# A streaming-encoder block: the scan stage's TensorE order written out by hand, with the entry reordered

## The chip, the core and the metric

The kernel runs on one core of one Trainium2 chip. The metric is the device time of one execution in microseconds (us): the median of three runs is given, and beside it one execution that was recorded by the hardware profiler. The engines are named as in the profile: PE is TensorE's matmul part, PEld its weight loads, DVE is VectorE, ACT is ScalarE, POOL is GpSimd, and SP is the engine whose queue issues all DMA transfers of this kernel. Each engine executes its own instructions in the order of the program; semaphores hold an instruction back until what it reads or overwrites is ready.

## The reference

One layer on 512 tokens of 1024 channels, all in float32:

- h is a layer norm of x. One projection of h gives z (2048 columns), xbc (3072), dt (32), q (1024), ckv (256), the index query (512), index key (64) and index weight (8), and two gates (1024 each).
- Branch A, the scan. xbc passes a causal depthwise convolution of four taps and SiLU, and is split into xs (32 heads of 64), B and C (4 groups of 128 states). The scan is done in chunks: the product of C and B inside a chunk is weighted by decays exp(a_i - a_j) and applied to xs; chunk states B·xs are carried on with a decay and read by C. The result plus D·xs is gated with SiLU(z), normalised over each group (RMS), and projected to 1024 (w_br_ssd).
- Branch B, the attention. A score of index queries and index keys selects the 128 best keys of each token; 16 heads attend to these keys through a shared latent of 256, with a relative bias.
- Both branches are gated and summed, projected (w_out), added to h and normalised; a convolutional FFN of 2 x 2816 columns and a last layer norm follow.

## The kernel before

**Precision.** A projection in float32 is made of three matmuls on values split in two parts: hi·hi, lo·hi and hi·lo, where hi is the value rounded to the type fp32r and lo the rest. One instruction of 128x128 weights and 512 columns stands for one such product. A weight tile of 128x1024 (one load, 512 KB) is split by ACT (`whi`, L190) and DVE (`wlo`, L191) after its DMA. A projection of 128 output channels over 8 k-tiles of h is so 24 matmuls of 512 columns into one PSUM bank (`proj`, L228). The matmuls inside the scan itself are plain float32 and have 128 columns or one.

**PSUM.** There are eight banks: three `acc` for projections, two `tr` for transposes, and `a`, `b`, `c` for the rest.

**Entry.** Four tiles of x (128 tokens each) are loaded, their mean and variance taken on DVE, normalised (tiles 0 and 1 by two ACT instructions each, L343 and L344; tiles 2 and 3 by DVE, L348), transposed on PE, evicted with the layer norm's gain (L360, L362), and split into `hhi` (L368) and `hlo` (L369). Three projections begin as soon as parts of h are there: the small columns (104: index key, dt, index weight) and the first two tiles of the index query (`his`, L381). A helper `put` fixes the order of DVE, ACT and POOL here, and `chain` fixes PE's order.

**The scan stage** (L702 to L729). After the decays, the latents and the index keys, `scores` multiplies 24 times (3 token blocks, 8 heads) index queries by keys. Then `ssd_in(g)` projects B, C and four xs tiles of a group g with their convolutions; `ssd_core(g, j)` does the scan of one xs tile (two heads): transposes of xs (L597), chunk states (`sp`, L608), the carry on DVE (`pv`, L615), decays on ACT (eight Relu of 128 columns, L621, and one Exp), their product with the masked C·B (L624), the states' part (`yo`, L627, bank `b`), the part within the chunk (`yd`, L631, bank `c`: eight matmuls of 64 output rows, heads in turn on the two halves), and the sum on DVE and POOL (L634 to L636); then z is projected and gates the result. `ssd_norm` and `ssd_out` finish a group while the next is under way. The loops only give the order of the program text: a list scheduler at build time orders each engine's instructions by that text and by its own estimate of when each is ready. Between a projection's 24 matmuls it may so put matmuls of the scan.

**Selection.** `select(i)` (L523) finds the 128 best keys of a token block by 16 rounds of a maximum and a replacement on DVE; its first instruction may not stand ahead of the result `v` of a core named in `PINS`: (2, 2), (3, 1), (3, 3).

After the scan stage come the first pair's q and k, four gates, the last group's output projection (these three in the scheduler's order), the attention in a PE order written by hand, and the output projection and the FFN.

## Time and profile before

| | |
|---|---|
| median of 3 runs | 1116.24 us (1116.22 to 1117.04) |
| the profiled execution | 1116.95 us |
| its span, first to last instruction | 1115.2 us |
| PE busy | 1092.7 us (98%), 5420 matmul instructions |
| PEld busy | 900.8 us (81%) |
| DVE busy | 780.7 us (70%) |
| ACT busy | 479.8 us (43%) |
| POOL busy | 175.3 us (16%) |
| DMA | 125.62 MB, mean 113 GB/s |

The profile's busy time of an engine is the union of its instructions' durations. A matmul's end is modelled, and consecutive ones overlap; the distance from one start to the next is what a matmul costs in a stream. An idle time is given with what ended it ("<-"). PEclk is the share of full clock that TensorE was granted.

### The profile page before, as it was taken

Reading aid. Unit: us, or ns where it says so; the run is one execution under the profiler, and the core shown is the slowest. Engines: PE = TensorE matmul, PEld = TensorE weight load, DVE = VectorE, ACT = ScalarE, POOL = GpSimd, SP = SyncE. Lnnn points to the kernel's source line nnn. Section 1 sums busy time; section 2 is a strip of 40 time slices with the busy share of each in tenths; the row PEclk is TensorE's granted clock in tenths of the full one; section 3 lists DMA queues with packets and bytes.
Section 4 is the critical chain, followed back from the end, with each engine's and each line's share of the span. In section 5 each row is a group of like instructions: output and inputs, shape, how many; then the busy total and the mean of one; then the engine's idle time right before and its main releaser. Section 6 shows DMA issues by size and latency. Waiting matters only on the chain.

```text
span 1115.2 us, 14590 instructions
## 1 busy us (share of the span) xinstructions
PE 1092.7 (98%) x5420; PEld 900.8 (81%) x5420; DVE 780.7 (70%) x1409; ACT 479.8 (43%) x825; POOL 175.3 (16%) x177
## 2 busy tenths in 40 slices
PE   7999999999999999999999999999999999999996
PEld 5888788878888888887777778888888888888885
DVE  7769678856799799758989848666656565542227
ACT  5475646554553423255555524215444444432220
POOL 3000023112211132013232432130000000000002
PEclk9999999999999999999999999999999999999999
DMA  6542343373333332422322356502232233333232
GB/s 234 169 137 78 103 131 116 107 226 132 119 109 123 103 106 85 146 81 71 90 67 75 116 175 187 187 1 95 95 95 95 95 97 101 105 95 95 95 95 76
DMA packets 41640, 125.62 MB, mean 113 GB/s; under 512 B 4720, under 2 KB 9120, under 8 KB 41568
## 3 DMA queue, kind: packets, MB, share of 16 engines
q1 hardware_dynamic: 41568, 124.68, 35.0%
q8 instruction: 43, 0.70, 0.3%
q14 instruction: 29, 0.24, 0.1%
HBM read 118.21 MB, written 9.59 MB: 115 GB/s over the span
## 4 chain that ended last, share of the span: by engine, by line
PE 86%; DVE 6%; DMA 4%; issue 2%; ACT 1%; POOL 1%; SPq 0%; DVEq 0%; ACTq 0%; POOLq 0%
PE pacc L217 52%; PE pc L217 5%; PE pacc L241 5%; PE ptr L241 4%; PE pa L217 3%; PE pb L217 3%; PE pb L241 2%; PE pc L241 2%; PE pa L241 2%; DMA rs_d<-rb_d 1%; DVE wlo L191 1%; PE pc L631 1%; PE ptr L217 1%; DMA G<-ac_d 1%; DMA prow<-in_prow_dram 1%
## 5 line engine op out<-in xcount | busy, mean ns | idle before, releaser
L191 DVE TENSOR_TENSOR wlo<-wraw,whi 128x1024 fp32r<-128x1024 f32 x159 | 203.4, 1279 | 155.3 <-ACT whi L190 154.6
L190 ACT ACTIVATE whi<-wraw 128x1024 fp32r<-128x1024 f32 x159 | 168.0, 1057 | 211.1 <-PE pacc L217 135.1
L217 PE MATMUL pacc<-hhi,whi 128*128 128x512 f32 (+1 forms) x536 | 217.4, 406 | 0.8 <-ACT hhi L368 0.8
L217 PE MATMUL pacc<-hlo,whi 128*128 128x512 f32 (+1 forms) x536 | 212.0, 395 | 1.6 <-DVE hlo L369 1.6
L217 PE MATMUL pacc<-hhi,wlo 128*128 128x512 f32 (+1 forms) x536 | 209.1, 392 | 0.2 <-DVE wlo L191 0.2
L217 PEld LDWEIGHTS pacc<-hlo,whi 128*128 128x128 f32 (+1 forms) x536 | 100.7, 188 | 25.0 <-DVE hlo L369 3.3
L217 PEld LDWEIGHTS pacc<-hhi,whi 128*128 128x128 f32 (+1 forms) x536 | 101.1, 189 | 21.6 <-issue 2.6
L217 PEld LDWEIGHTS pacc<-hhi,wlo 128*128 128x128 f32 (+1 forms) x536 | 100.8, 188 | 19.6 <-issue 0.6
L172 POOL TENSOR_TENSOR rs_y<-rs_v,mhalf 128x1 f32<-128x1 f32 (+1 forms) x14 | 14.0, 1000 | 463.2 <-DVE rs_v L170 463.2
L217 PE MATMUL pacc<-h1hi,wlo 128*128 128x512 f32 (+1 forms) x216 | 79.0, 366 | 0.0
L217 PE MATMUL pacc<-h1hi,whi 128*128 128x512 f32 (+1 forms) x216 | 78.9, 366 | 0.0
L217 PE MATMUL pacc<-h1lo,whi 128*128 128x512 f32 (+1 forms) x216 | 78.7, 366 | 0.0
L814 POOL TENSOR_TENSOR tm<-mask,toe 128x128 f32<-128x128 f32 (+1 forms) x64 | 44.5, 699 | 156.8 <-DVE mn L825 94.5
L636 POOL TENSOR_TENSOR v<-v,eaB 128x384 f32<-128x384 f32 x16 | 22.8, 1424 | 230.4 <-DVE eaB L634 152.6
L548 DVE SCALAR_TENSOR_TENSOR cv<-pacc,cwb,cv 128x509 f32<-128x509 f32 (+2 forms) x72 | 53.3, 741 | 0.6
L621 ACT ACTIVATE G<-G,acT 128x128 f32<-128x128 f32 x128 | 39.4, 389 | 31.5 <-DMA G<-ac_d 30.1
L828 ACT ACTIVATE l<-l,mn 128x128 f32<-128x128 f32 (+1 forms) x64 | 35.7, 558 | 36.9 <-DVE mn L825 35.8
L217 PE MATMUL pacc<-yhi,whi 128*128 128x512 f32 x128 | 51.1, 400 | 0.0
L217 PE MATMUL pacc<-yhi,wlo 128*128 128x512 f32 x128 | 50.2, 392 | 0.0
L217 PE MATMUL pacc<-ylo,whi 128*128 128x512 f32 x128 | 50.1, 392 | 0.0
L217 PEld LDWEIGHTS pacc<-h1hi,whi 128*128 128x128 f32 x216 | 40.8, 189 | 6.7
L217 PEld LDWEIGHTS pacc<-h1hi,wlo 128*128 128x128 f32 x216 | 40.7, 189 | 6.6
(476 smaller groups left out, 2275.0 us busy)
## 6 DMA issues: line engine op xcount, KB each, us to landing
wraw<-in_w_up_dram SPq DMA_DIRECT2D x44, 512.0 KB, 3.5
wraw<-in_w_xbc_dram SPq DMA_DIRECT2D x24, 512.0 KB, 3.5
wraw<-in_w_down_dram SPq DMA_DIRECT2D x22, 512.0 KB, 3.4
wraw<-in_w_z_dram SPq DMA_DIRECT2D x16, 512.0 KB, 3.5
G<-ac_d SPq DMA_DIRECT2D x16, 512.0 KB, 4.0
wraw<-in_w_br_ssd_dram SPq DMA_DIRECT2D x16, 512.0 KB, 3.5
eaB<-ea_d SPq DMA_DIRECT2D x32, 128.0 KB, 3.1
wraw<-in_w_ga_dram SPq DMA_DIRECT2D x8, 512.0 KB, 3.5
```

The costliest lines, as they stand in the source:

```text
L172: last_pow[0] = nc.gpsimd.tensor_tensor(y, v, mhalf[:, :n], OP.pow)
L190: nc.scalar.activation(hi[:, :cols], raw[:, :cols], AF.Copy)
L191: nc.vector.tensor_tensor(lo[:, :cols], raw[:, :cols], hi[:, :cols].bitcast(F32), OP.subtract)
L217: pe(nc.tensor.matmul(p, a, b, start=start, stop=stop).ins)
L241: nc.tensor.matmul(p, x[a][:, tok(i)], w[b][h], start=first and j == 0, stop=last and j == 2)
L548: nc.vector.scalar_tensor_tensor(y[:, d:], p[:, :T - d], cwb[:, 24 * k + c:24 * k + c + 1], y[:, d:], OP.mult, OP.add)
L621: nc.scalar.activation(G[:, h, c], G[:, h, c], AF.Relu, bias=acT[:, c, h0 + h:h0 + h + 1], scale=-1.0)
L631: nc.tensor.matmul(yd[h * 64:(h + 1) * 64, tok(c)], xd[:, c, h], G[:, h, c], start=True, stop=True)
L636: nc.gpsimd.tensor_tensor(v[:, P:], v[:, P:], eaB[:, P:], OP.add)
L814: nc.gpsimd.tensor_tensor(tm[:, :K - f], maskt[i][:, f:], self.toe[:, 2 * P - K + f:], OP.add)
L828: nc.scalar.activation(l[:, :K], l[:, :K], AF.Exp, bias=self.mn[:, ic], scale=-1.0, accum_out=self.sm[:, ic])
```

## The change

**Entry.** The variance's constant and the negated mean times the root of tiles 0 to 2 move from DVE to POOL; tiles 0 to 2 are each normalised by one ACT instruction, tile 3 by DVE. The warming matmuls of PE use a tile of ones instead of x: 20 ahead of the first transposes, two after each of tiles 0 and 1 (before: six on x[1], two on x[2]; a float32 matmul shows as two records). The small weights are padded from 104 to 128 columns for each k-tile (the load grows from 416 to 512 KB) and split in two halves on ACT. The orders of ACT and DVE and of the first three projections on PE are rewritten.

**Scan stage.** The loop over `ssd_core` is replaced by generators for the projections (one step is one k-tile: three matmuls) and by lists of items that are called after given steps; `chain` is on, so PE's order is the order of these calls. Items come for two cores j and j + 1 at once (`pair`). There are nine runs: the first has no pair (48 steps), then come 40, 48, four of 56, 40 and 32; together 432 steps. The decays of a core are issued in four pieces of two Relu (`ssd_g`); the transposes of B (`ssd_b`) stand apart from the product C·B (`ssd_cb`); the parts within the chunk of both cores are one item (`ssd_d`, banks `c` and `a`); the root of a norm (`rms_root`, bank `b`) stands apart from its broadcast (`rms_bcast`, bank `c`). The 24 score products are items too and use the two `tr` banks. Two gates (`out_ga`) move from the last group to the first run. The bias rows' loads (`t5_load`) and product (`t5_rows`) are items of the first run of group 1. The selections' first instructions may follow the cores (1, 3), (2, 3) and (3, 1).

```diff
-PINS = ((2, 2), (3, 1), (3, 3))
-IN_STEPS = (1, 1, 2, 2)
-OUT_STEPS = (0, 0, 0, 2, 4)
...
-        put(V, nc.vector.tensor_scalar(v, mv[:, 1:2], 1.0, EPS, OP.mult, OP.add))
+        if i < 3:
+            put(G, nc.gpsimd.tensor_scalar(v, mv[:, 1:2], 1.0, EPS, OP.mult, OP.add))
+        else:
+            put(V, nc.vector.tensor_scalar(v, mv[:, 1:2], 1.0, EPS, OP.mult, OP.add))
         last_pow[0] = put(G, nc.gpsimd.tensor_tensor(y, v, mhalf[:, :1], OP.pow))
-        if i < 2:
-            put(V, nc.vector.tensor_scalar(nm, mv[:, 0:1], -1.0, None, OP.mult))
+        if i < 3:
+            put(G, nc.gpsimd.tensor_scalar(nm, mv[:, 0:1], y, -1.0, OP.mult, OP.mult))
...
+    def warm(n):
         for _ in range(n):
-            mm(trs[7][:, :P], ident, xt[i][:, :P], start=True, stop=True)
+            mm(trs[7][:, 3 * P:], ones, ones, start=True, stop=True)
+
+    warm(20)
     for i, t in enumerate(xt):
+        if i < 3:
+            put(S, nc.scalar.activation(t, t, AF.Identity, bias=nms[i], scale=rss[i]))
+        else:
+            for j in range(2):
+                x_ = t[:, half_of(j)]
+                put(V, nc.vector.tensor_scalar(x_, x_, mvs[i][:, 0:1], rss[i], OP.subtract, OP.mult))
+        for k in range(KD):
+            mm_t(trs[k][:, tok(i)], t[:, tok(k)], ident)
         if i < 2:
-            put(S, nc.scalar.activation(t, t, AF.Identity, bias=nms[i]))
-            put(S, nc.scalar.activation(t, t, AF.Copy, scale=rss[i]))
-        for j in range(2):
-            x_ = t[:, half_of(j)]
-            if i > 1:
-                put(V, nc.vector.tensor_scalar(x_, x_, mvs[i][:, 0:1], rss[i], OP.subtract, OP.mult))
-            for k in range(4 * j, 4 * j + 4):
-                mm_t(trs[k][:, tok(i)], t[:, tok(k)], ident)
+            warm(2)
         nc.sync.dma_start(htok_d[:, i], t)
...
+    w_hi(0, slice(0, 4))
+    for k in range(2):
         evict(k)
-        evict(k + 1)
-        for j in (k, k + 1):
-            put(S, nc.scalar.activation(hhi[:, j], hfs[j], AF.Copy))
-            put(V, nc.vector.tensor_tensor(hlo[:, j], hfs[j], hhi[:, j].bitcast(F32), OP.subtract))
-        if k < 6:
-            w_hi(1 + k // 2)
-    for j in range(4):
+    h_hi(0)
+    evict(2)
+    h_lo(0)
+    h_hi(1)
+    h_lo(1)
+    w_hi(1)
+    h_hi(2)
+    evict(4)
+    h_lo(2)
+    evict(3)
+    h_hi(3)
+    evict(6)
+    h_lo(3)
+    w_hi(0, slice(4, KD))
+    w_lo(0)
+    h_hi(4)
+    h_lo(4)
+    w_hi(2)
+    evict(5)
+    evict(7)
+    for k in (5, 6, 7):
+        h_hi(k)
+        h_lo(k)
+    w_hi(3)
+    for j in range(1, 4):
         w_lo(j)
...
+    his(0, 0, 1)
+    his(1, 0, 1)
+    for k in (2, 3):
+        his(0, k)
+        his(1, k)
+    los(0, 0, 1, 2, 3)
+    his(0, 4)
+    his(1, 4)
+    his(2, 0, 1, 2)
+    his(0, 5)
+    his(1, 5)
+    his(2, 3, 4, 5)
+    for k in (6, 7):
+        for j in range(3):
+            his(j, k)
+    los(0, 4, 5, 6, 7)
+    los(1, *range(KD))
+    los(2, *range(KD))
     chain[0] = False
...
-                p = any_tile("abc")
-                nc.tensor.matmul(p[:, :K], qi[h][:, tok(i - 1)], khi[:, :K], start=True, stop=False)
-                nc.tensor.matmul(p[:, :K], qi[h][:, tok(i - 1)], klo[:, :K], start=False, stop=True)
+                p = tr_tile()
+                mm(p[:, :K], qi[h][:, tok(i - 1)], khi[:, :K], start=True, stop=False)
+                mm(p[:, :K], qi[h][:, tok(i - 1)], klo[:, :K], start=False, stop=True)
...
+    def in_b(g):
 
         bc = wt("k4", [P, 2, T], "bc")
-        BT, CT = bc[:, 0], bc[:, 1]
-        st_ = {"CT": CT, "xs": []}
-        sins[g] = st_
-        conv_silu(BT, proj_h(w_("w_xbc", 16 + g)), 16 + g)
+        sins[g] = {"BT": bc[:, 0], "CT": bc[:, 1], "xs": [], "core": [], "v": []}
+        p = acc_tile()
+        yield from steps(p, w_("w_xbc", 16 + g), hT)
+        conv_silu(bc[:, 0], p, 16 + g)
         yield
-        conv_silu(CT, proj_h(w_("w_xbc", 20 + g)), 20 + g)
...
+    def in_z(g, j):
+
+        p = acc_tile()
+        yield from steps(p, w_("w_z", 4 * g + j), hT)
+        zs = wt("m2", [P, T], "zs")
+        nc.scalar.activation(zs, p, AF.Tanh, scale=0.5)
+        nc.vector.scalar_tensor_tensor(zs, zs, 1.0, p, OP.add, OP.mult)
+        sins[g]["z", j] = zs
+        ssd_gate(g, j)
+        yield
...
+    def ssd_g(g, j, n):
+
+        G = sins[g]["core", j][2]
+        h, c0 = n // 2, n % 2 * 2
+        q = 2 * (4 * g + j) + h
+        for c in range(c0, c0 + 2):
+            nc.scalar.activation(G[:, h, c], G[:, h, c], AF.Relu, bias=acT[:, c, q:q + 1], scale=-1.0)
+        if n == 3:
+            nc.scalar.activation(G, G, AF.Exp, scale=-1.0)
...
+    def ssd_y(g, j):
...
+            mm(yo[:, tok(c)], pv[:, c - 1], s_["CT"][:, tok(c)], start=True, stop=True)
         nc.vector.tensor_tensor(eaB[:, P:], yo[:, P:], eaB[:, P:], OP.mult)
...
+    def ssd_d(g, js):
+
+        s_ = sins[g]
+        yds = [ps(t) for t in "ca"]
+        for j, yd in zip(js, yds):
+            xd, xdd, G, eaB, pv = s_["core", j]
+            for c in range(NT):
+                for h in range(2):
+                    mm(yd[h * 64:(h + 1) * 64, tok(c)], xd[:, c, h], G[:, h, c], start=True, stop=True)
+        for j, yd in zip(js, yds):
+            q = 4 * g + j
+            eaB = s_["core", j][3]
+            v = wt("v", [P, T], "v")
+            last_v[0] = nc.vector.scalar_tensor_tensor(v, s_["xs"][j], Dv[:, q:q + 1], yd, OP.mult, OP.add)
+            nc.gpsimd.tensor_tensor(v[:, P:], v[:, P:], eaB[:, P:], OP.add)
+            s_["v"].append(v)
+            ssd_gate(g, j)
...
+    AT = (2, 6, 13, 18, 28, 32, 40)
...
+    sins, last_v, pins, ga = {}, [None], [], SSD_GATES
+    score = scores()
+
+    def run(projs, items):
+
+        k = 0
+        for p in projs:
+            for _ in p:
+                for f, *args in items.get(k, ()):
+                    f(*args)
+                k += 1
+        assert k > max(items), (k, items)
+
+    def pair(g, j, at, more=(), root=10, norm=20):
+
+        items = {}
+        more = [*more]
+        if g and not j:
+            more += [(root, ssd_root, g - 1), (norm, ssd_norm, g - 1)]
+        x0, x1, s0, s1, y0, y1, d = at
+        for n in range(4):
+            more += [(x0 + 3 + 2 * n, ssd_g, g, j, n), (x1 + 4 + 2 * n, ssd_g, g, j + 1, n)]
+        more += [(x0, ssd_x, g, j), (x1, ssd_x, g, j + 1), (s0, ssd_s, g, j, "a"), (s1, ssd_s, g, j + 1, "b"),
+                 (s1 + 2, ssd_gm, g, j), (s1 + 5, ssd_gm, g, j + 1),
+                 (y0, ssd_y, g, j), (y1, ssd_y, g, j + 1), (d, ssd_d, g, (j, j + 1))]
+        for k, *f in more:
+            items.setdefault(k, []).append(f)
+        return items
+
+    def scored(*ks):
+        return [(k, next, score, None) for k in ks]
+
+    def pin():
+        pins.append(last_v[0])
+
+    chain[0], last_pe[0] = True, None
+    first_items = {k: [f] for k, *f in scored(*range(33, 48, 2))}
+    first_items[26] = [(ssd_b, 0)]
+    first_items[44] = [(ssd_cb, 0)]
+    run([in_b(0), in_c(0), out_ga(0), in_x(0, 0), out_ga(1), in_x(0, 1)], first_items)
+    run([in_x(0, 2), in_z(0, 0), in_x(0, 3), in_z(0, 1), in_b(1)],
+        pair(0, 0, (2, 10, 14, 19, 26, 29, 36), scored(*range(1, 40, 3))))
+    run([in_x(1, 0), in_x(1, 1), in_z(0, 2), in_c(1), in_z(0, 3), in_x(1, 2)],
+        pair(0, 2, AT, [*scored(3, 5, 7), (21, ssd_b, 1)]))
+    for g in (1, 2):
+        run([in_x(g, 3), in_z(g, 0), in_b(g + 1), in_z(g, 1), out_br(g - 1, 0), out_br(g - 1, 1), in_c(g + 1)],
+            pair(g, 0, AT, [(1, ssd_cb, 1), (18, t5_load), (46, t5_rows)] if g == 1 else ()))
+        run([in_x(g + 1, 0), in_z(g, 2), out_br(g - 1, 2), in_x(g + 1, 1), in_z(g, 3), out_br(g - 1, 3),
+             in_x(g + 1, 2)], pair(g, 2, AT, [(11, ssd_b, g + 1), (21, ssd_cb, g + 1), (42, pin)]))
+    run([in_x(3, 3), in_z(3, 0), in_z(3, 1), out_br(2, 0), out_br(2, 1)],
+        pair(3, 0, (0, 4, 11, 16, 25, 28, 36), [(37, pin)], norm=18))
+    run([in_z(3, 2), in_z(3, 3), out_br(2, 2), out_br(2, 3)],
+        pair(3, 2, (0, 3, 9, 14, 23, 25, 30)))
+    chain[0] = False
```

Left out of the diff: the same move of code from `ssd_in` and `ssd_core` into `in_c`, `in_x`, `out_br`, `out_ga`, `ssd_b`, `ssd_cb`, `ssd_x`, `ssd_gm`, `ssd_s` and `ssd_gate`, with `mm` and `mm_t` in place of direct matmul and transpose calls; `steps` moved up; the padding of the small weights.

## Rows read from the trace of the kernel before

**Rows 1.** The page, part 4: shares of the chain that ended last.
```profile
PE 86%; DVE 6%; DMA 4%; issue 2%; ACT 1%; POOL 1%; SPq 0%; DVEq 0%; ACTq 0%; POOLq 0%
```
**Rows 2.** Stretches: length, busy us and count of each engine, PEclk, DMA.
```profile
56.00:448.00 392.00, 389.06 (x2064) 321.30 (x2063) 314.60 (x544) 196.68 (x366) 73.53 (x55) 1.00 0.38 119
308.00:420.00 112.00, 112.00 (x612) 92.80 (x611) 102.68 (x212) 45.35 (x83) 23.50 (x18) 1.00 0.36 112
```
**Rows 3.** The chain that ended last, in the FFN: start us, us, what.
```profile
785.51 5.44 PE pacc L217 x24
```
**Rows 4.** PE's groups from 56 to 448 us: form, count, busy, mean ns, idle before.
```profile
L217 PE MATMUL pacc<-hhi,whi 128*128 128x512 f32 x358 | 142.4, 398 | 0.0
...
L217 PE MATMUL pacc<-yhi,whi 128*128 128x512 f32 x96 | 38.8, 404 | 0.0
...
L631 PE MATMUL pc<-G,xd 128*64 128x128 f32 x256 | 19.7, 281 | 0.2 <-DVE v L635 0.2
L627 PE MATMUL pb<-bc,pv 128*128 128x128 f32 x96 | 17.8, 282 | 1.6 <-DVE pv L615 1.3 <-ACT pv L611 0.3
L608 PE MATMUL pa<-xdd,bt 128*128 128x128 f32 x96 | 13.3, 275 | 0.0
L597 PE MATMUL ptr<-ident,xs 128*128 128x128 f32 x64 | 9.8, 275 | 0.0
```
**Rows 5.** PE in order of time, one core's matmuls kept together: start, us, what.
```profile
408.18 0.83 PE L608 MATMUL pa<-xdd,bt 128*128 128x128 f32 x6
408.94 1.09 PE L631 MATMUL pc<-G,xd 128*64 128x128 f32 x16
409.96 0.50 PE L217 MATMUL pacc<-hhi,whi 128*128 128x512 f32 x1
410.30 0.39 PE L217 MATMUL pacc<-hhi,wlo 128*128 128x512 f32 x1
```
**Rows 6.** PE in order of time, pieces of several cores mixed.
```profile
233.98 0.87 PE L631 MATMUL pc<-G,xd 128*64 128x128 f32 x10
234.78 0.49 PE L627 MATMUL pb<-bc,pv 128*128 128x128 f32 x2
...
236.65 0.43 PE L631 MATMUL pc<-G,xd 128*64 128x128 f32 x2
...
237.36 0.40 PE L217 MATMUL pacc<-hhi,wlo 128*128 128x512 f32 x1
```
**Rows 7.** PE's waits from 56 to 448 us: total us, times, longest.
```profile
PE pb L627 <- DVE pv L615: 1.3, 1, 1.3
...
PE pc L631 <- DVE v L635: 0.2, 1, 0.2
```
**Rows 8.** Stretches of the entry, columns as in rows 2.
```profile
11.00:14.80 3.80, 3.07 (x26) 2.60 (x24) 2.97 (x7) 2.31 (x5) 0.90 (x1) 1.00 1.00 304
14.80:17.90 3.10, 1.40 (x4) 0.70 (x5) 2.04 (x5) 2.15 (x4) 1.98 (x1) 0.99 1.03 421
17.90:21.30 3.40, 3.40 (x10) 2.41 (x9) 2.37 (x4) 3.02 (x5) 3.40 (x1) 0.50 0.37 152
```
**Rows 9.** The entry in order of time: start, us, what, idle before and what ended it.
```profile
15.81 0.39 DVE L400 COPY Dv<-prow 64x16 f32<-64x16 f32 x2 [1.66 <-DMA prow<-in_prow_dram]
...
16.98 0.48 PE L217 MATMUL pacc<-hlo,whi 128*104 128x512 f32 x1 [1.63 <-DVE hlo L369]
...
32.88 0.33 PE L217 MATMUL pb<-hhi,wlo 128*128 128x384 f32 x1
```
**Rows 10.** Durations ns min/median/max, first and last start, of single lines.
```profile
L191 DVE TENSOR_TENSOR wlo<-wraw,whi x159: 1203/1226/2312, 32.1 to 1071.4; 128x1024 fp32r<-128x1024 f32 x159
L548 DVE SCALAR_TENSOR_TENSOR cv<-pacc,cwb,cv x72: 679/743/751, 62.4 to 354.3; 128x511 f32<-128x511 f32 x24, 128x510 f32<-128x510 f32 x24, 128x509 f32<-128x509 f32 x24
L634 DVE TENSOR_TENSOR eaB<-pb,eaB x16: 542/549/559, 134.5 to 418.7; 128x384 f32<-128x384 f32 x16
```
**Rows 11.** DMA issues from 200 to 260 us: count, KB each, us to landing.
```profile
rs_d<-rb_d SPq DMA_DIRECT2D x1, 3072.0 KB, 16.4
```

More of the change, by code (lines that the diff above doesn't have):

```diff
@@ L252, in ln_stats, with rms_root, rms_bcast, steps @@
         return mv, rsqrt_small(mv[:, 1:2], 1.0, EPS, 1, i)
-    def rms_bcast(sqs, n):
-        s4 = ps("a")
+    def rms_root(sqs, n):
+        s4 = ps("b")
         for i in range(NT):
             for j, sq in enumerate(sqs):
-                nc.tensor.matmul(s4[:, i:i + 1], sq[:, tok(i)], ones[:, 0:1],
-                                 start=j == 0, stop=j == len(sqs) - 1)
-        r = rsqrt_small(s4[:, :NT], 1.0 / n, EPS, NT)
-        rb = ps("b")
+                mm(s4[:, i:i + 1], sq[:, tok(i)], ones[:, 0:1], start=j == 0, stop=j == len(sqs) - 1)
+        return rsqrt_small(s4[:, :NT], 1.0 / n, EPS, NT)
+    def rms_bcast(r):
+        rb = ps("c")
         for i in range(NT):
-            nc.tensor.transpose(rb[:, tok(i)], r[:, i:i + 1].to_broadcast([P, P]), ident)
+            mm_t(rb[:, tok(i)], r[:, i:i + 1].to_broadcast([P, P]), ident)
         return rb
+    def steps(p, w, rhs, off=0):
+        for k in range(len(rhs)):
+            proj(p, w, rhs, off=off, part=(k, k + 1))
+            if k < len(rhs) - 1:
+                yield
     def stack_parts(even, odd, p, scale, cols):
@@ L326, in block_kernel, with small, w_hi @@
     wq = [whls[0]] + [[y[:, half_of2(j)] for y in y8s] for j in range(2)] + [whls[1]]
-    wcols = [slice(0, KD * 104)] + [slice(0, D)] * 3
-    def w_hi(j):
-        put(S, nc.scalar.activation(wq[j][0][:, wcols[j]], raws[j][:, wcols[j]], AF.Copy))
+    def small(t, ks=slice(0, KD)):
+        return t.rearrange("p (k m) -> p k m", m=P)[:, ks, :104]
+    def w_hi(j, ks=slice(0, KD)):
+        a, b = (small(t, ks) if j == 0 else t for t in (wq[j][0], raws[j]))
+        put(S, nc.scalar.activation(a, b, AF.Copy))
@@ new lines, in out_br, with out_ga @@
+    def out_br(g, s):
+        w = w_("w_br_ssd", 4 * g + s)
+        for j in range(2):
+            n = 2 * s + j
+            p = acc_tile()
+            yield from steps(p, w, sins[g]["y"], off=T * j)
+            if g == 0:
+                nc.scalar.activation(mssd[:, n], p, AF.Copy)
+            else:
+                nc.vector.tensor_tensor(mssd[:, n], mssd[:, n], p, OP.add)
+            yield
+    def out_ga(n):
+        p = acc_tile()
+        yield from steps(p, w_("w_ga", n), hT)
+        sg = wt("m2", [P, T], "sga")
+        nc.scalar.activation(sg, p, AF.Tanh, scale=0.5)
+        nc.sync.dma_start(ga_d[n], sg)
+        yield
@@ L604, in ssd_core, with ssd_gm, ssd_s @@
         nc.vector.tensor_tensor(xd, tr4, dt[:, :, hs2, None].to_broadcast(X4), OP.mult)
[L606 removed]
+        s_["core", j] = [xd, xdd, G, eaB, None]
+    def ssd_g(g, j, n):
[6 more added lines that the diff above has]
+            nc.scalar.activation(G, G, AF.Exp, scale=-1.0)
+    def ssd_gm(g, j):
+        G = sins[g]["core", j][2]
+        nc.vector.tensor_tensor(G, G, sins[g]["cbm"][:, None].to_broadcast([P, 2, NT, P]), OP.mult)
+    def ssd_s(g, j, bank):
+        s_ = sins[g]
+        xd, xdd, G, eaB, _ = s_["core", j]
+        h0 = 2 * (4 * g + j)
+        sp = v3(ps(bank), NT - 1)
         for c in range(NT - 1):
[L608 to L609 removed]
+            mm(sp[:, c], s_["bt"][:, c], xdd[:, c].rearrange("p h d -> p (h d)"), start=True, stop=True)
         pv = wt("m2", [P, NT - 1, P], "pv")
@@ L617, in ssd_core @@
                                                OP.mult, OP.add)
-        for h in range(2):
-            for c in range(NT):
-                nc.scalar.activation(G[:, h, c], G[:, h, c], AF.Relu, bias=acT[:, c, h0 + h:h0 + h + 1],
-                                     scale=-1.0)
-        nc.scalar.activation(G, G, AF.Exp, scale=-1.0)
-        nc.vector.tensor_tensor(G, G, cbm[:, None].to_broadcast([P, 2, NT, P]), OP.mult)
+        s_["core", j][4] = pv
+    def ssd_y(g, j):
+        s_ = sins[g]
+        xd, xdd, G, eaB, pv = s_["core", j]
@@ L749, in block_kernel @@
     wk_ = [None]
-    def steps(p, w, rhs, off=0):
-        for k in range(len(rhs)):
-            proj(p, w, rhs, off=off, part=(k, k + 1))
-            if k < len(rhs) - 1:
-                yield
     def pair_in(r, res):
```

177 lines of the change are left out of this document (69 added, 108 removed).

## The prediction

> **What bounds the kernel now.** I read the shares of the chain that ended last first: 86% of it is PE, 6% DVE [rows 1]. So the time is PE's, and the question is how much of PE's time is work. Busy shares can't tell that, since a matmul's end is modelled; distances between starts can. In the FFN the chain holds 24 projection matmuls of 512 columns in 5.44 us, 0.2267 us each, and that stretch has nothing else [rows 3]. This is the pace to which I hold the rest.
>
> From 56 to 448 us, where the scan lies, PE is "busy" 389 of 392 us [rows 2]. Its groups there give the work at pace [rows 4]: 3 x 358 + 3 x 96 + 6 = 1368 projection matmuls x 0.2267 = 310.1 us (the six belong to the attention's values). The 48 score matmuls, 16 each of 512, 384 and 256 columns, take 8.3 us by their columns. Six full-width matmuls of 128 columns start 0.11 us apart: from 408.18 to 408.94 is 0.76 us, of which some 0.10 is the change to half width that follows [rows 5]. So L608 and L627, 192 records, are 21.0 us; L597's 64 and some 72 like them (transposes of B, C·B products, norms) 14.8 us. The half-width matmuls of L631 run in pairs: 16 records take 1.02 us with their exit [rows 5], 8 x 0.103 = 0.82 without; 256 records are 13.2 us. Some 62 records of one column and others are put at 0.11, 6.8 us. The sum is 374.2 us. 392.0 - 374.2 = 17.8 us is lost in this stage.
>
> Where? Waits that the profile names are small: six of 0.2 to 1.3 us, 2.9 us together [rows 7]. The rest is lost at changes of form. The cheapest case is a core's pieces kept together: after L631 the second projection matmul comes 1.36 us after 408.94, so the half-width group costs 1.36 - 0.82 - 0.23 = 0.31 us at its end and about 0.10 at its start, 0.41 [rows 5]. The dear case is mixed: from 233.98 to 237.36 is 3.38 us, for 16 half-width records (0.82), ten full-width (1.1) and one projection matmul (0.23); 1.2 us is lost in one core [rows 6].
>
> The entry has its own loss. PE waits 1.63 us for the first lo part of h, because DVE stands 1.66 us at two small copies whose row arrives by DMA at 15.8 [rows 9]. PE is busy 1.40 of 3.10 us there, and in the next 3.40 us it is granted half the clock [rows 8].
>
> **The change part by part.** The sum is made on the profiled 1116.95 us; the median is 0.71 us lower, and I take that off at the end.
>
> *Entry: -3.0 us.* The first three projections are 24 matmuls of 512 columns and 48 of 384, 24 x 0.2267 + 48 x 0.173 = 13.7 us (0.173 is the pace by columns). They now run from 14.87 to 32.88 [rows 9], 18.0 us: 4.3 are lost, of them 1.63 the wait and 1.7 the half clock (half of 3.40). Without the copies' 1.66 us in front of it the first lo part comes near 15.3 instead of 16.98, and one ACT pass for each of three tiles brings the tiles no later than now. After that every k-tile still passes DVE (an eviction or none, then lo), and the order written lets PE catch up with it: I leave 1.2 us of waits. 4.3 - 1.2 = 3.1, less 0.1 for the larger first load. Bounds: 4.5 gained (all losses, and 0.2 of an earlier start) to 0.5 lost (the copies again stand ahead of the first lo, the clock falls as before, and the 96 KB more, at the 304 to 421 GB/s of these stretches, delay the row by 0.3). What follows is bound by PE, so what is won here stays won. The warming matmuls, 48 records for 16, lie in PE's idle time before x is normalised and cost nothing; if the first 40 ran at half pace throughout, 0.22 us each or 8.8 us, they could hold the first transposes up by some tenths.
>
> The Trainium skill ("TensorE: Matmul & The Clock Gate", Part 4: PE-mode transpose) says that transposes don't count as PE work for the clock. By it the clock would fall during the transposes and the first projections run at half pace for 3.4 us, 1.7 us more, 1108.3 in all. This trace speaks against it: the stretch that holds nothing but transposes has PEclk 1.00, and so has the next [rows 8].
>
> *Scan, fewer and purer groups: -9.4 us.* The instructions stay the same; only their order on PE changes. The half-width matmuls now come in eight groups of 64 records (two cores each) instead of sixteen or more: 8 x 0.41 = 3.3 us stays. Full-width groups are 16 each of `ssd_x`, `ssd_s` and `ssd_y`, eight for B and C·B, four others: 60. Each costs between nothing and the 0.09 us that the six L608 leave over (0.76 - 0.67) [rows 5]; I take 0.06, 3.6 us. The latents and decays, not touched, keep about 1.5. So 8.4 of 17.8 stay. Bounds: 3.3 saved (only the halving of the half-width groups) to 11 (full-width groups for nothing).
>
> *Scan, new waits: +2.4 us of those 9.4.* The old 17.8 holds 2.9 us of waits, and the new order has its own. A step is 3 x 0.2267 = 0.68 us. Most slacks are wide: states at 13 and their readers at 28 lie 10 us apart, decays at 5 to 16 and their readers at 40 over 16 us; a root at 10 comes 26 steps, 17.7 us, after the last `ssd_d` in runs of 56, which covers POOL's sums. Two are narrow. `ssd_y` of both cores writes bank `b`, so the second (4 steps, 2.7 us later; 3 and 2 in the last two runs) needs DVE's 0.55 us product of the first [rows 10] to be over. And in the first run of group 3 the norm has 6 steps, 4.1 us, before the projection that reads it. On DVE such a product can stand behind a 1.2 us weight split and convolution taps of 0.74 [rows 10]. DVE is 80% busy in the stage (314.6 of 392) and 92% between 308 and 420 [rows 2]. Bounds: none to 19 us (the slower rival). I take what waits cost before less the decays' half microsecond, 2.4.
>
> *ACT's decays in four pieces, C's product apart, score products among the steps, two gates moved: 0.* These don't change the count of any engine's work; ACT is busy 197 of 392 us [rows 2], and a piece of two Relu holds the next weight split up less than eight did. If that cover were gone, it would show as PE waiting for wlo. The score products take the `tr` banks in turn with the transposes and are freed by a short ACT pass three steps ahead of the next: nothing.
>
> *Transfers: 0.* `G` and `eaB` of a pair are asked for once the pair before has given its buffers up, 18 steps (12 us) ahead, and a weight load behind them on SP waits with them. The 3 MB spread of the bias rows takes 16.4 us [rows 11]; it stands in the middle of the stage before and after the change, behind `G` of the pair that was last asked for. Weights are ahead by two projections, 11 us, and PE consumes three in that time; bounds nothing to 3 us lost.
>
> *Selections sooner: 0.* They are DVE work that moves from the crowded end (92% [rows 2]) to an earlier stretch. The attention does not begin sooner, as PE has gates and the last output projection to do until then.
>
> Sum: 1116.95 - 3.0 - 9.4 + 2.4 = 1106.95, and 1106.2 as a median; **forecast 1106.2 us**, own range 1102 to 1110.5.
>
> **The rivals.**
> - *A price for each group.* If a change of form costs what it does whatever its length, only the eight half-width groups that vanish are won: 1116.2 - 3.0 - 3.3 = 1110 us. For: the number of groups is much the same. Against: the 1.2 us of the mixed case against 0.41 [rows 5, 6].
> - *Waits eat the scan's gain.* The narrow slacks and a DVE at 92% cost 9 us instead of 2.4: 1113 us. For: DVE is close to full where the selections run. Against: with DVE at 92% the present order has no wait over 1.3 us in the whole stage [rows 7].
> - *The entry does not do what it says.* The copies wait for their row again and the clock falls: 1109 us. For: nothing in the new order of DVE fixes the copies' place.
> - *Better on both.* All of the entry's bounds, no waits: 1101 us.
> - *Slower: one late operand holds all of PE.* Place: the second `ssd_y` of each pair. If DVE reaches the first's product behind two splits and three taps (2.4 + 2.2 us, then 0.55 for itself) [rows 10], it is over 5.1 us after it is due, 2.4 past the 2.7 us of slack; in eight pairs PE stands 19 us: 1116.2 - 3.0 - 9.4 + 19 + 2.4 = 1125 us. It decides from 1.2 us of waiting a pair. For: no other matmul may go ahead. Against: DVE's order is made with the same lists, and lets the product through as soon as it is due. The skill's same page (Part 2) states that matmuls keep the order of the program, only weight loads being pulled ahead; the starts in these rows agree [rows 5, 6].
>
> **How the numbers follow.** Forecast 0.56, price for each group 0.12, waits 0.10, entry 0.08, better 0.06, slower 0.08. About 0.2%, 2.2 us, is what a measurement can tell here: faster is under 1114.0. The forecast, the group price, the entry, the better case and a third of the waits are faster, 0.84; the rest of the waits, 0.07, is no change; slower 0.09, with a little for waits beyond theirs. The range 1100 to 1115 leaves out the slower case and a little below.
>
> **What would show it.** In the changed trace PE's first half-width group should have 64 records in one piece and lose about 0.4 us; the work at pace should stay at 374 us and the stage end some 7 us earlier relative to its start. The first matmul on a lo part should start near 15.3 us, with no stretch at half clock after 14 us, and the first three projections end near 30. PE's waits in the scan should sum to 2 to 3 us. I am wrong if PE waits over 8 us there (DVE products or norms named), if pure groups cost as much as mixed ones, or if the entry ends after 32 us.

## The result, and the profile after

The changed kernel takes 1125.6 us (1125.2 to 1126.3) against 1116.2 us (1115.3 to 1117.0) for the kernel before: ratio 1.0085, 95% interval 1.0068 to 1.0103. It is 9.4 us slower; forecast was 10 us faster. The spans of the profiled executions say the same, 1123.5 us against 1115.2, +8.3.

Where the time went is read first from the chain that ended last (part 4 of the page of the changed kernel). Of before it was 86% PE [rows 1]:

```profile
PE 76%; issue 8%; DVE 8%; ACT 3%; DMA 3%; POOL 1%; SPq 0%; DVEq 0%; POOLq 0%; ACTq 0%
```

PE has lost the chain to others: it stands and waits. Stretches of the changed kernel, columns as in rows 2: three of the entry [rows 8], the scan stage and its crowded part [rows 2], then two pairs, each a wait and what follows it.

```profile
11.00:14.80 3.80, 2.91 (x23) 2.32 (x21) 3.10 (x5) 2.84 (x6) 0.07 (x1) 1.00 1.03 336
14.80:17.90 3.10, 2.66 (x11) 1.88 (x12) 3.06 (x8) 3.07 (x6) 3.03 (x1) 1.00 1.03 422
17.90:21.30 3.40, 3.03 (x14) 1.90 (x13) 3.40 (x6) 3.37 (x7) 2.90 (x1) 1.00 0.61 207
54.00:456.00 402.00, 388.86 (x2060) 320.78 (x2059) 315.43 (x561) 194.90 (x363) 65.75 (x56) 0.99 0.37 117
308.00:420.00 112.00, 108.38 (x563) 89.24 (x560) 92.81 (x169) 52.55 (x103) 21.89 (x19) 0.97 0.35 113
136.00:141.00 5.00, 1.50 (x8) 0.92 (x6) 4.42 (x5) 5.00 (x13) 0.47 (x1) 1.00 0.29 107
141.70:145.10 3.40, 3.40 (x9) 2.65 (x8) 3.40 (x5) 3.34 (x5) 0.64 (x1) 0.50 0.02 5
384.00:387.40 3.40, 0.99 (x4) 0.36 (x3) 3.40 (x9) 3.40 (x6) 0.00 (x0) 1.00 0.02 6
387.50:394.20 6.70, 5.49 (x16) 4.09 (x17) 6.60 (x15) 0.00 (x0) 0.00 (x0) 0.50 0.27 81
```

The entry has lost its stretch at half clock. The scan stage holds the same work (2060 records, 388.9 us busy, against 2064 and 389.1) and is 10 us longer. PE is idle for 3.5 us before 141 and most of 384 to 387.4, and behind both it is granted half the clock, 1.2 GHz, which the scan before never had. PE's waits there (total us, times, longest), against six of 2.9 us together before [rows 7]:

```profile
PE pb L214 <- DVE eaB L744: 3.5, 2, 1.9
PE ptr L217 <- ACT rel L511: 3.5, 1, 3.5
PE pacc L214 <- DVE ylo L174: 3.3, 2, 2.1
PE ptr L217 <- DVE xs L603: 1.4, 1, 1.4
...
```

With four more of 0.2 to 0.5 us they sum to 13.1 us in ten waits. (`eaB` is a core's states' part after its product on DVE, which frees bank `b`; `rel` a score after its Relu, which frees a `tr` bank; `yhi` and `ylo` the two parts of a normed group; `zs` the gate made of z; `pv` the carried states.) The longest is explained by ACT's order, shown with the end of PE's score product of step 3 (start, us, what, idle before):

```profile
132.06 2.45 ACT L711 ACTIVATE G<-G,acT 128x128 f32<-128x128 f32 x8 [1.41 <-DMA G<-ac_d]
134.42 0.61 ACT L773 ACTIVATE ssum<-v 128x512 f32<-128x512 f32 x1
134.58 0.40 PE L214 MATMUL ptr<-klo,qi 128*128 128x512 f32 x1
134.94 1.04 ACT L187 ACTIVATE whi<-wraw 128x1024 fp32r<-128x1024 f32 x1
135.89 0.76 ACT L597 ACTIVATE cv<-pacc,cwb 128x512 f32<-128x512 f32 x1
136.55 2.44 ACT L711 ACTIVATE G<-G,acT 128x128 f32<-128x128 f32 x8
138.89 1.04 ACT L713 ACTIVATE G<-G 128x1024 f32<-128x1024 f32 x1
139.84 0.61 ACT L776 ACTIVATE sq<-v 128x512 f32<-128x512 f32 x1
140.36 1.06 ACT L511 ACTIVATE rel<-ptr 128x512 f32<-128x512 f32 x2
```

The score products of steps 3 and 5 each hold a `tr` bank until ACT's Relu (L511) has read it. On ACT these Relu stand behind the decays of both cores, which the scheduler put eight in a row and not in quarters, the first behind a DMA that ACT waited 1.41 us for. The product of step 3 is over at 134.98 us and its Relu begins at 140.36: a weight split, a convolution tap, eight Relu and an Exp of the decays and a square stand in between, 5.4 us. The transposes of x at step 6 need one of the banks; so does everything behind them, as PE's order is fixed.

DVE's order at the waits for `ylo` (the same view):

```profile
383.06 2.71 DVE L792 SCALAR_TENSOR_TENSOR v<-v,ngh,pc 128x512 f32<-128x512 f32 x4
385.70 0.07 DVE L584 MATCH_VALUE_LOAD mask<-m,mask 128x8 f32 x1
385.77 0.53 DVE L584 MATCH_REPLACE8 mask<-m,mask 128x384 f32<-128x384 f32 x1
386.23 0.45 DVE L732 SCALAR_TENSOR_TENSOR pv<-pv,cd,pb 128x64 f32<-128x64 f32 x2
386.61 0.68 DVE L174 TENSOR_TENSOR ylo<-v,yhi 128x512 fp32r<-128x512 f32 x1
387.21 1.21 DVE L188 TENSOR_TENSOR wlo<-wraw,whi 128x1024 fp32r<-128x1024 f32 x1
388.34 0.68 DVE L637 SCALAR_TENSOR_TENSOR zs<-zs,pacc 128x512 f32<-128x512 f32 x1
388.94 0.55 DVE L583 MAX8 m<-mask 128x8 f32<-128x384 f32 x1
389.41 1.88 DVE L174 TENSOR_TENSOR ylo<-v,yhi 128x512 fp32r<-128x512 f32 x3
```

Between the norm's products and the first `ylo` stand a replacement of the selection and `pv`; between that and the next three a weight split, z and the selection's next maximum. PE took up the first `ylo` at 387.33, the second at 390.13.

The entry in order of time, against 16.98 and 32.88 [rows 9]:

```profile
14.96 0.48 PE L214 MATMUL pacc<-hlo,whi 128*104 128x512 f32 x1 [0.24 <-DVE hlo L380]
...
30.68 0.33 PE L214 MATMUL pb<-hhi,wlo 128*128 128x384 f32 x1
```

From there to the attention's first product (478.8 us before, 487.1 after) both kernels run 2315 recorded matmuls. Before:

```profile
32.90:478.80 445.90, 442.96 (x2315) 367.34 (x2314) 353.84 (x621) 213.31 (x389) 75.18 (x56) 1.00 0.39 122
```

After:

```profile
30.60:487.10 456.50, 443.36 (x2315) 367.30 (x2314) 346.61 (x618) 212.39 (x387) 65.75 (x56) 0.99 0.37 118
```

Idle time rose from 2.94 to 13.14 us, +10.2. PE was busy at half clock for 3.4 + 5.5 us, which is 4.5 us more than at full clock. Busy time rose by only 0.4, so the rest of it fell by 4.1. With 2.2 won in the entry: -2.2 + 10.2 + 4.5 - 4.1 = +8.4 for +8.3 measured. From 487 us on nothing changes but the shift.

### The profile page after: what moved, and what is told of

The parts are those of the page before. It is cut to its first block, busy times and chain, and to the rows that moved or that the text cites. A ratio compares the mean times of both kernels' runs of the same rounds, so it can differ in the third digit from the quotient of the medians.

```text
span 1123.5 us, 14635 instructions
## 1 busy us (share of the span) xinstructions
PE 1095.4 (98%) x5452; PEld 903.1 (80%) x5452; DVE 773.2 (69%) x1402; ACT 479.1 (43%) x825; POOL 167.0 (15%) x183
## 4 chain that ended last, share of the span: by engine, by line
PE 76%; issue 8%; DVE 8%; ACT 3%; DMA 3%; POOL 1%; SPq 0%; DVEq 0%; POOLq 0%; ACTq 0%
PE pacc L214 43%; PE pc L214 6%; PE pacc L238 5%; PE pb L214 5%; PE ptr L238 4%; PE pa L214 3%; DMA G<-ac_d 2%; PE ptr L214 2%; PE pb L238 2%; PE pc L238 2%; PE pa L238 2%; DVE wlo L188 2%; ACT G L711 2%; ACT whi L187 1%; PE pa L217 1%
## 5 line engine op out<-in xcount | busy, mean ns | idle before, releaser
L188 DVE TENSOR_TENSOR wlo<-wraw,whi 128x1024 fp32r<-128x1024 f32 x159 | 198.6, 1249 | 177.6 <-ACT whi L187 177.2
L214 PE MATMUL pacc<-hhi,whi 128*128 128x512 f32 (+1 forms) x536 | 220.3, 411 | 1.0 <-ACT hhi L377 0.8
L169 POOL TENSOR_TENSOR rs_y<-rs_v,mhalf 128x1 f32<-128x1 f32 (+1 forms) x14 | 14.9, 1064 | 483.1 <-DVE rs_v L167 483.1
L600 DVE SCALAR_TENSOR_TENSOR cv<-pacc,cwb,cv 128x511 f32<-128x511 f32 (+2 forms) x72 | 53.1, 742 | 0.5
L760 POOL TENSOR_TENSOR v<-v,eaB 128x384 f32<-128x384 f32 x16 | 17.5, 1109 | 235.5 <-DVE v L759 174.1
```

The source lines that it names most:

```text
L169: last_pow[0] = nc.gpsimd.tensor_tensor(y, v, mhalf[:, :n], OP.pow)
L188: nc.vector.tensor_tensor(lo[:, :cols], raw[:, :cols], hi[:, :cols].bitcast(F32), OP.subtract)
L214: pe(nc.tensor.matmul(p, a, b, start=start, stop=stop).ins)
L600: nc.vector.scalar_tensor_tensor(y[:, d:], p[:, :T - d], cwb[:, 24 * k + c:24 * k + c + 1], y[:, d:], OP.mult, OP.add)
L760: nc.gpsimd.tensor_tensor(v[:, P:], v[:, P:], eaB[:, P:], OP.add)
```

## The experiments

Times are medians; the ratio is to the kernel before, run beside each, 0.001 being 1.1 us. A difference of two ratios carries both intervals: it is known to some 2.4 us where the change is one of the two, to 1.7 us between the kernel with all moves and one with a place put back. A row of an experiment is from its own profile.

**The entry alone** (old scan, new entry: the diff's hunks up to `his` and `los`, and `w_small`).

> The kernel before with the new entry alone (normalisation on ScalarE in one step, dummy matmuls from the start, padded w_small, the new order of the first three projections); the scan is the old one. The theory (T) is that the entry gained and the scan's waits lost: in the profile after, the first projections end 2.3 us sooner than before, so T expects about 1114 us (1113 to 1115). The rival that the entry is part of the loss (it changes which loads and weight splits come when, and the scan starts badly) expects 1116 or more. The prediction's own term was -3.0, 1113.2.

1112.75 us, 0.9983 (0.9974 to 0.9992): 1.9 us faster. The entry gained; the whole loss, some 11 us, is the scan's.

**Selections as late as before.**
```
-... (21, ssd_cb, g + 1), (42, pin)]))
+... (21, ssd_cb, g + 1), *[(42, pin)] * (g == 2)]))
-        pair(3, 2, (0, 3, 9, 14, 23, 25, 30)))
+        pair(3, 2, (0, 3, 9, 14, 23, 25, 30), [(31, pin)]))
```


> The changed kernel with the three key selections allowed as late as before (after the ends of (2,3), (3,1) and (3,3) in place of (1,3), (2,3) and (3,1)). T says that the selections are not the cause: the long waits are a transpose behind ScalarE's decays (3.5 us at 141), the norm's ylo (3.6 us at 384 to 391) and the second ssd_y's bank (3.5 us at 300 and 428), each followed or not by half the clock; T expects 1124 to 1127, no long wait gone, though the ylo wait may shrink as rounds of the selection stand between the norm's operations on DVE. The rival that the sooner selections crowd DVE expects the waits at 300, 387 and 428 to go with them and the half clock behind 387: 1125.6 - 7.1 - 3.4 = 1115.

1121.3 us, 1.0057 (1.0045 to 1.0070): 3.1 us less than the change. Between the two: one wait for eaB and one for ylo went, the wait for rel stayed (3.6 us). I had called the selections innocent; they are a part.

**Score products behind the transposes.**
```
-        pair(0, 2, AT, [*scored(3, 5, 7), (21, ssd_b, 1)]))
+        pair(0, 2, AT, [*scored(9, 12, 15), (21, ssd_b, 1)]))
```


> The changed kernel with the last three score products of the third run at steps 9, 12 and 15 in place of 3, 5 and 7, so that both transposes of x come before them and take no bank that waits for ScalarE. T expects the 3.5 us wait at 141 to go, and the 3.4 us at half the clock behind it (1.7 us of time): 1125.6 - 5.2 = 1120.4 (1119.5 to 1122). The rival that ScalarE or DVE is simply full there expects the wait to come back within the same run at another operand (the score products themselves, ssd_s, or the decays' product): 1124 to 1126.

1121.0 us, 1.0058 (1.0045 to 1.0070), 3.0 less. The wait for rel and the half clock behind it are gone; compared projection by projection, PE is 5.1 us ahead at 155 us, behind the moved products (5.2 expected), and 4.3 ahead at 428: new waits in the last run gave some back:

```profile
PE pacc L214 <- DVE zs L637: 1.2, 1, 1.2
PE pb L214 <- DVE pv L732: 1.0, 1, 1.0
```

**The idle time filled.** In two places dummies of `ones` by `ones`, 32 each, ahead of the instruction that waits:
```
+    def fill_in(tile):
+        p = tile()
+        for _ in range(32):
+            mm(p[:, :P], ones, ones, start=True, stop=True)
...
+ (6, fill_in, lambda: ps("c"))          # run of (0,2)
+ (23, fill_in, tr_tile)                 # run of (3,0)
```


> The changed kernel with 32 dummy products of 128 columns (3.5 us) just ahead of the transpose that waits 3.5 us at 141, and 32 ahead of out_br's first product of group 2, which waits 3.6 us in all at 384 to 391. Nothing else is moved. The dummies stand where TensorE stood idle, so they cost nothing if that idle time is there anyway. If the clock halves because TensorE stood still, it stays full in both places: 10.2 us at half the clock give back 5.1 us, 1120.5 (1119.5 to 1122). If the half clock has another cause, or a wait only moves behind the dummies, nothing comes back: 1125 to 1133.

1125.9 us, 1.0099 (1.0085 to 1.0113), with the clock full through the scan. My size was wrong. PE in order of time:

```profile
137.26 7.31 PE L214 MATMUL pc<-ones 128*128 128x128 f32 x64
```

A float32 dummy is two records, so each place got 7.1 us and not 3.5: 7 us of added work hid what the clock gave back. With 16:

> The fill again with its right size: a dummy product of 128 columns took 0.22 us (two records of 0.11 us each), so that 32 of them stood for 7.1 us and not 3.5 in each place; they added 7.1 us of work in all beyond the idle time, and the time stayed at 1125.9 with the clock full. With 16 in each place (3.6 us) the theory that the half clock follows the idle time and costs half of itself expects the clock full (0.998) and 1125.6 - 5.1 = 1120.5 (1119.5 to 1122). The rival that the full clock gave nothing and the longer fill was hidden otherwise expects 1125 to 1126.

1120.5 us, 1.0046 (1.0033 to 1.0058), 4.4 to 5.1 us less than the change. The same stretches as above, now without half clock:

```profile
141.50:145.00 3.50, 3.50 (x17) 2.88 (x16) 3.40 (x4) 3.39 (x5) 0.76 (x1) 1.00 0.00 0
...
387.50:394.00 6.50, 6.50 (x35) 5.56 (x36) 6.39 (x15) 0.50 (x1) 0.00 (x0) 1.00 0.17 69
```

So work that computes nothing, put where PE stood still, makes the kernel faster: the half clock follows the idle time and is a cost of its own.

**More steps for the norm.**
```
-    run([in_x(3, 3), in_z(3, 0), in_z(3, 1), out_br(2, 0), out_br(2, 1)],
+    run([in_x(3, 3), in_z(3, 0), in_z(3, 1), in_z(3, 2), out_br(2, 0)],
-    run([in_z(3, 2), in_z(3, 3), out_br(2, 2), out_br(2, 3)],
+    run([out_br(2, 1), in_z(3, 3), out_br(2, 2), out_br(2, 3)],
```


> The changed kernel with z(3,2)'s projection ahead of out_br of group 2 (in the run of (3,0)) and out_br's second weight one run later, so that the norm of group 2 has 14 steps, as in the other groups, and not 6. The theory that the fixed order is tight at this place expects the waits for yhi and ylo (3.6 us at 384 to 391) and the 6.8 us at half the clock behind them (3.4 us) to go: 1125.6 - 7 = 1118.6 (1117.5 to 1121). The theory that DVE is full in the last two runs of the scan expects part of it back as new waits further on (zs, pv, eaB, as 1.8 us came back at 416 to 424 when the scores were moved): 1120.5 to 1124.

1123.4 us, 1.0074 (1.0062 to 1.0086), 1.2 less, which is within the uncertainty. The profile is of an execution of 1119.5 us, the fastest of six, and has no half clock in the scan; in it the ylo waits are gone, and waits for eaB (now 4.8 us in three) and pv (1.8) came in their place.

**The second `ssd_y` in bank a.**
```
-                 (y0, ssd_y, g, j), (y1, ssd_y, g, j + 1), ...
+                 (y0, ssd_y, g, j, "b"), (y1, ssd_y, g, j + 1, "a"), ...
```


> The changed kernel with the second ssd_y of a pair in bank a (free since its ssd_s) in place of bank b, where it waits for DVE to have read the first one. The theory that the bank is the cause expects both waits (1.65 us at 300, 1.86 us at 428) to go: 1125.6 - 3.5 = 1122.1 (1121 to 1123.5). The rival that DVE is late and the bank only shows it expects waits for pv of the second core, or for eaB at ssd_d, in their place: 1124.5 to 1126.

1124.3 us, 1.0083 (1.0070 to 1.0096): no change that can be told. The profile is of an execution of 1127.1 us, the slowest of six, with 17.1 us at half clock in the scan against 10.3 in the change. No wait for eaB is left, and these rows grew or are new:

```profile
PE pacc L214 <- DVE zs L637: 2.1, 1, 2.1
...
PE pacc L214 <- ACT yhi L173: 1.3, 1, 1.3
```

**All moves together**, with the second x transposes of the first pair 2 steps later and its states 1 step later (`(2, 12, 15, 20, 26, 29, 36)`).

> The moves together: score products at steps 9, 12, 15; the second x transposes of the first pair 2 steps later; the second ssd_y in bank a; z(3,2) ahead of out_br of group 2; the selections allowed as late as before the change. The theory (a handful of narrow places in the fixed order, DVE's selections making the last ones worse) expects nearly all of 12.6 us of waits and 5.1 us at half the clock back: 1125.6 - 15 = 1110.5 (1108 to 1113), faster than the kernel before and than its entry alone (1114). The rival that DVE's whole load sets the pace of the scan whatever the order expects new waits for 5 us and more: 1114 to 1118.

1111.35 us, 0.9968 (0.9956 to 0.9981). That is 13.0 us less than the change by the ratios, where the four tried alone gave 3.1 + 3.0 + 1.2 + 0.2 = 7.5 (14.3 against 12.4 by the medians; the x transposes were not tried alone). The change's own ratio stands in each of the four, so 7.5 is known to some 8 us only: that together they gain more than one by one is not shown. No half clock is left before 1105 us. The same stretch as above:

```profile
30.50:473.10 442.60, 438.54 (x2316) 365.05 (x2315) 341.71 (x612) 212.49 (x387) 66.29 (x55) 1.00 0.38 121
```

4.1 us of idle time, and 4.4 us less busy time than before.

A place mended alone shows what is left after the next narrow place has taken its share, as the new waits above do. So each was put back alone into this order, undoing one of the edits above:

> The kernel with all moves together (1111.35 us), but with the selections allowed sooner again, as in the change. It asks what the sooner selections cost where the rest of the order is clean. The prediction's term was 0; the late selections alone won about 3 us on the changed kernel. The theory that selections take DVE in front of operands that TensorE waits for expects 1 to 4 us more, 1112.5 to 1115.5, with waits for DVE at 290 to 390 named in the profile. The rival that they only hurt where a place was narrow anyway expects no change: 1110.8 to 1112.

1115.9 us, 1.0003 (0.9994 to 1.0012): the sooner selections cost 3.9 us. The stretch in which the first one now runs, in this kernel:

```profile
250.00:300.00 50.00, 47.60 (x245) 38.63 (x244) 44.80 (x96) 23.70 (x45) 8.64 (x7) 0.97 0.33 106
```

and with all moves:

```profile
250.00:300.00 50.00, 50.00 (x288) 41.57 (x288) 35.97 (x56) 25.45 (x46) 8.69 (x8) 1.00 0.35 110
```

DVE has 9 us more to do, and PE loses 2.4 us and full clock: it waits 2.04 us for zs at 296.2 us and has half the clock behind that, to 299.8.

> All moves together, but the second ssd_y in bank b again. On the changed kernel bank a took both named waits away (3.5 us) and the time moved by about 1 us at most, since later waits grew. If the bank costs what was named, 1 to 3.5 us come back here: 1112.4 to 1115. If with less crowded DVE the product of the first core is ready in time, nothing: 1110.8 to 1112.

1113.4 us, 0.9986 (0.9977 to 0.9995): bank b costs 2.0 us.

> All moves together, but the norm of group 2 with 6 steps again (z(3,2) and out_br as in the change). If 6 steps are too few whatever DVE has to do besides, 3 us of waits and up to 3.4 us for half the clock come back: 1114 to 1118. If the crowding by the selections made them too few, under 1.5 us: 1111 to 1113.

1113.7 us, 0.9990 (0.9981 to 0.9998): the short norm costs 2.5 us.

> All moves together, but the last three score products at steps 3, 5 and 7 of the third run again. The theory (a tr bank behind ScalarE's decays) expects the 3.5 us wait and mostly the 1.7 us for the clock: 1111.35 + 5.2 = 1116.5 (1114.5 to 1117). If the rest of the order makes up for it by slack later on, 1111 to 1113.

1116.05 us, 1.0011 (1.0002 to 1.0019): the scores cost 4.8 us, wait (3.3) and half clock included.

> All moves together, but the second x transposes of the first pair at step 10 again. The theory expects the 1.4 us wait for xs: 1112.8 (1112 to 1113.3). If nothing behind it is late for it, 1110.8 to 1111.8.

1112.4 us, 0.9983 (0.9974 to 0.9991): the early transposes cost 1.7 us.

The five sum to 14.9 us; together they gave 13.0 by the ratios, 14.3 by the medians. The ratio of all moves stands in each of the five, so their sum is known to some 7 us: that they add up fits, and is not shown more closely. Each has its own row in its profile: the waits that came back are zs 2.8 us in place of 0.3, eaB 3.3, ylo 1.9, rel 3.3 and xs 1.4.

**What is left.** Two tries, first the norm at 16:
```
-        pair(3, 0, (0, 4, 11, 16, 25, 28, 36), [(37, pin)], norm=18))
+        pair(3, 0, (0, 4, 11, 16, 27, 31, 36), [(37, pin)], norm=16))
```
and root 13 in place of 10 in the runs of (1,0) and (2,0).

> All moves together and two more steps: in the run of (3,0) both ssd_y 2 and 3 steps later and the norm 2 steps sooner (pv stood behind the norm's four operations there, 1.1 us), and the roots in the runs of (1,0) and (2,0) 3 steps later (0.6 us for ssum). The theory of narrow places expects those 1.7 us back: 1109.7 (1109 to 1111). The rival that DVE's load decides expects them again elsewhere: 1111 to 1112.5.

1110.5 us, 0.9966 (0.9953 to 0.9979): no change that can be told. pv waited 2.3 us, as the norm's operations now reached DVE with the states. With `norm=20`, behind the states:

> All moves together; both ssd_y of (3,0) 2 and 3 steps later; the norm of group 2 at step 20 of that run, behind the states and no longer at the same step; the roots in the runs of (1,0) and (2,0) 3 steps later. In the first try (norm at 16) pv stood behind the norm's work on DVE for 2.3 us and the clock halved for 3.4. With the states first pv should be ready: 1111.35 - 1.1 - 0.6 = 1109.6 (1108.5 to 1110.5). If DVE is simply full there, 1110.5 to 1112.

1108.7 us, 0.9948 (0.9936 to 0.9959): 5.8 us faster than the kernel before and the best of all. All that PE waits for in its scan stage:

```profile
PE pc L556 <- DVE acT L554: 0.5, 1, 0.5
```

Just behind the stage, at 443.4 us, it still waits 1.3 us for a weight's lo part.

**More half-width groups**, on all moves:
```
-                 ... (d, ssd_d, g, (j, j + 1))]
+                 ... (d - 1, ssd_d, g, (j,), "c"), (d, ssd_d, g, (j + 1,), "a")]
```


> All moves together, but ssd_d's half-width products of a pair's two cores one step apart: sixteen groups of 32 records in place of eight of 64, the same matmuls. In the profile of all moves a half-width group lost 0.48 us beside its matmuls, whatever stood next to it. If that is a price for each group: 1111.35 + 8 x 0.48 = 1115.2 (1114.5 to 1116). If the loss goes with the number of half-width matmuls, no change: 1110.8 to 1112.

1114.55 us, 0.9997 (0.9988 to 1.0005): 3.2 us more, 0.40 for each added group. (A pair has 32 such records, 16 for each core: the 64 of the prediction and the figures of this expectation are twice too many. The number of groups, eight and sixteen, is right.) PE in order of time with all moves:

```profile
163.43 0.39 PE L214 MATMUL pacc<-hlo,whi 128*128 128x512 f32 x1
163.75 1.09 PE L214 MATMUL pc<-G,xd 128*64 128x128 f32 x16
164.67 1.04 PE L214 MATMUL pa<-G,xd 128*64 128x128 f32 x16
165.64 0.50 PE L214 MATMUL pacc<-hhi,whi 128*128 128x512 f32 x1
165.98 0.40 PE L214 MATMUL pacc<-hhi,wlo 128*128 128x512 f32 x1
```

and split:

```profile
162.73 0.39 PE L214 MATMUL pacc<-hlo,whi 128*128 128x512 f32 x1
163.05 1.09 PE L214 MATMUL pc<-G,xd 128*64 128x128 f32 x16
164.07 0.50 PE L214 MATMUL pacc<-hhi,whi 128*128 128x512 f32 x1
...
164.96 1.09 PE L214 MATMUL pa<-G,xd 128*64 128x128 f32 x16
165.99 0.50 PE L214 MATMUL pacc<-hhi,whi 128*128 128x512 f32 x1
166.32 0.40 PE L214 MATMUL pacc<-hhi,wlo 128*128 128x512 f32 x1
```

From the first start to the last is 2.55 us, less 16 pairs of 0.103 and two projections of 0.227 is 0.45 lost; split it is 3.59, less 1.65 and five projections (1.13), 0.81.

## Why the prediction was wrong

The terms on the spans, each as forecast and as measured; the scan's -9.4 held the 2.9 us of old waits, so it is -6.5 and the waits -0.5:

| term | forecast | measured | error |
|---|---|---|---|
| entry | -3.0 | -2.2 | 0.8 |
| changes of form | -6.5 | -4.1 | 2.4 |
| waits of PE in the scan | -0.5 | +10.2 | 10.7 |
| half clock behind them | none | +4.5 | 4.5 |
| sum | -10.0 | +8.4 | 18.4 |

**The step that failed is "Scan, new waits: +2.4 us".** I took what waits cost before for what they would cost in an order written without an estimate of when each operand is ready. In both kernels PE's order is fixed when the program is built, and a late operand holds all of PE (1.3 us for pv before, 3.5 us for rel after). But before, the list scheduler placed each matmul by its estimate of when its operands are there: with the old scan order and the new entry the waits are 2.2 us, with the written order 13.1. PE's waits are 13.1 us, over the 8 that I named as proof against me. My bound of 19 held, but what I took lay near its lower end, and the clock was in no term.

Point by point in that step:

- The two narrow places that I named are there: the second `ssd_y` (2.0 us) and the norm with 6 steps (2.5 us).
- "The score products take the `tr` banks in turn ... and are freed by a short ACT pass: nothing" was wrong by 4.8 us. The pass is short, but it has a place in ACT's queue, and 5.4 us of other work, the decays above all, stood between it and its product. I counted ACT's load (197 of 392 us), and not what stands ahead on it.
- "Selections sooner: 0" was wrong by 3.9 us. I saw them leave the crowded end (92% of DVE became 83% from 308 to 420) and did not ask what they meet: the first selection the norm of group 1 and, in the same run, the second `ssd_y` of group 2's first pair (the wait at 300 us, which went when the selections were late), the second selection the norm of group 2 (384 to 391 us).
- The transposes at step 10 of the first pair (1.7 us) I did not see. Decays in four pieces did not come about where it mattered: at the wait for rel the scheduler put them eight in a row.

**The entry** went by its steps: the first lo part at 14.96 us (15.3 forecast), no half clock there, the first projections over at 30.7 (near 30), the copies of D no longer ahead of the first lo part. Waits of 0.2 to 0.8 us stayed, -2.2 in the profile, 1.9 by itself.

**Changes of form.** The mechanism and its price hold: 0.45 us lost at a half-width group (0.41 used), 0.40 for each group added. The gain was mis-sized: 4.1 us here, 4.4 with all moves, where 6.5 was forecast. PE's starts between the first projections and the attention say which item was too low (each record at the pace of its form, waits taken off; the parts overlap by up to 0.7 us). What is lost beside waits is 15.2 us before and 10.6 with all moves. Half-width groups lose 10.1 us in 18 groups before and 3.6 in eight after (3.3 forecast to stay). All other groups, the latents and decays among them, lose 3.2 us in 54 and 3.8 in 70 (3.6 and 1.5 forecast). The rest is spread thinly over the projections between the groups and went from 2.6 to 3.4 us. The forecast had no item for it, and took it for something that purer groups would save; what makes it up stays open.

**Slips in the sums.** A pair has 32 half-width records and not 64; the eight groups and their 256 records are right, so no term changes. The time by the rule on transposes comes to 1107.9 us and not 1108.3; the clock stayed full through the transposes and behind them (1.00 from 11.0 to 21.3 us).

**Transfers** cost nothing that the runs show, except that ACT stood 1.41 us for G ahead of the decays at the longest wait. In the later pairs it stood 4.2 to 8.4 us for G, and no wait of PE for the decays followed.

**The rivals.** The time was that of the slower one, 1125 us, for another reason: it put 19 us on the second `ssd_y`, and that costs 2.0. "One late operand holds all of PE" is right as a rule; it was five places and the clock, not one. "Waits eat the scan's gain" (1113) had the kind of loss and half its size. The price for each group is real (0.40 us); its sum, 3.3 us gained, lies nearer to the 4.1 to 4.4 measured than the forecast's 6.5, but for another reason: the half-width groups alone gave 6.5, and the other items took some back.

Without those places, and with two more moves, the change gains 5.8 us of the 10 forecast. The entry alone gives 1.9 of these 5.8 us (3.0 forecast).

## What to carry to other kernels

Where an engine's order is written by hand, a busy share says nothing on waits: for each operand, list what can stand ahead of its producer on that engine's queue and who holds the bank, and give it those microseconds of slack. A place mended alone can hand its wait to the next one (for the ylo waits, 1.8 us for pv and 1.3 more for eaB came here), so measure each by putting it back alone into an order that has none. And count a wait of some microseconds at more than its length if half clock can follow.
